# Where the adaLN weights of a two-layer diffusion step wait: rows of a transposed matrix leave the ring of raw weights for places of the general store

## The chip, the cores and the metric

The kernel runs on one core of one Trainium2 chip, in one launch. The metric is the device time of that core in microseconds (us). Five engines have queues of their own: TensorE (PE, matrix products; PEld is its weight load), VectorE (DVE), ScalarE (ACT), GpSimd (POOL) and SyncE (SP), which here does nothing but issue DMAs. Each engine takes its instructions strictly in the order in which they were written for it; an instruction that waits holds up all behind it on the same engine.

## The reference

One step of a hybrid backbone: two layers, model width 1024, 640 tokens (128 of a context, 512 of a latent grid). In each layer

```python
sh1, sc1, g1, sh2, sc2, g2 = split(silu(cond) @ w_ada + b_ada, 6)   # adaLN, two conditionings: c_ctx and c
z = (x * (1 + sc1) + sh1) @ w_in                     # one projection, cut into nine parts
r, s, n = retention(z), s5_ssm(z), attention(z)      # three mixers
m = (sig(ga) * (r @ wb[0]) + sig(gb) * (s @ wb[1]) + sig(gc) * (n @ wb[2])) @ w_o
x = layer_norm(alpha * x + g1 * m)
f = conv_ffn(x * (1 + sc2) + sh2)                    # up, 3-tap conv, gelu gate, down (D_FF = 2816)
x = layer_norm(alpha * x + g2 * f)
```

All of it is in float32. The six adaLN vectors of a layer are 48 columns of 128 numbers, for two conditionings each. The columns 0 to 15 (`sh1`, `sc1`) are needed first, 16 to 39 (`g1`, `sh2`, `sc2`) after the mixers, 40 to 47 (`g2`) after the ConvFFN.

## The kernel before, in words

**Products.** A float32 product is made as three products of rounded parts (hi·hi, hi·lo, lo·hi; `project`, L148). Weights come in tiles of 128 x 1024 (512 KB). Each is loaded by SP into one of four places of a ring called `raw` (L206), ACT rounds it to `hi` (L176), DVE subtracts to get `lo` (L177), and PE multiplies. `hi` and `lo` have rings of three places each.

**Units.** The program is a list of units that `run` goes through. A unit has slots (the weight tiles that it needs, in the order in which they are loaded) and `emit`, which writes its work. Loads are written ahead of their unit by the number of places in the ring, splits by two tiles.

**adaLN.** The first 16 columns of layer 0 are made by PE at the start. The rest is done on DVE beside other work: `ada_rows` takes 512 KB of the transposed matrix `w_adaT` (two columns of 128 outputs, one half of the 1024 inputs), and multiplies it with the conditioning, laid out as rows, in four `scalar_tensor_tensor` with a running sum (L308; the product itself goes to `junk` and is never read). There are 80 such units, spread between the products: 24 half-column units and 24 more beside the gates of each layer (L1284, L1302 and L1308 are the gate's evictions, branch products and gating), 8 and 8 for the last columns, 16 and 16 for the next layer's first columns beside layer 0's ConvFFN. Their slots are of kind `"raw"`: the tile stays in the ring of raw weights, between the weights of products, until DVE has read it four times.

**Conditioning rows.** `cond_rows` loads one half of both conditionings, broadcast over the partitions, as two tiles `crow` of 256 KB (L285), and makes silu of them with two tiles `crt` (tanh on ACT, L286; L287 and L288 on DVE). It is called again when the half changes.

**The store.** All other tiles live in a store of `NU` = 37 places of one size (`unit`, `free`): a list of idle places, taken from the front, given back at the end. A DMA into a place waits until the last reader of what lay there is done. `crow`, `crt`, the gates, q, k and v of the attention, its biases, and the tiles of the S5 preparation (`epm`, `ebe`, `eo` on POOL) come from it.

**What sets the order.** A scheduler orders each engine's instructions when the program is built; SP's queue is one in-order queue, and a DMA also waits for the one eight before it (eight semaphores take turns).

Of the kernel before, what the change touches and what calls it, by code (L numbers as in the profile page):

```python
# [11 lines left out]
FR = mybir.dt.float32r  # L12
I32 = mybir.dt.int32
AF = mybir.ActivationFunctionType
OP = mybir.AluOpType
AX = mybir.AxisListType

P = 128
# [62 lines left out]
class Kernel:  # L81
# [115 lines left out]
    def plan(s, units):  # L197
        s.units, s.cap = units, FIRST
        s.slots = [x for u in units for x in u["slots"]]
        s.raw, s.done, s.nraw, s.nsplit = {}, {}, 0, 0  # L200

    def load_to(s, n):
        while s.nraw < min(n, len(s.slots), s.cap):
            ap, kind, w = s.slots[s.nraw]
            t = s.wp.tile([P, 1024], FT, name=s.name("raw"), tag="raw", bufs=NRAW)
            s.nc.sync.dma_start(t[:, :w], ap)  # L206
            s.raw[s.nraw] = t
            s.nraw += 1

    def split_to(s, n):  # L210
        while s.nsplit < min(n, len(s.slots), s.cap):
            i = s.nsplit
            s.load_to(i + 1)
            t = s.raw.pop(i)
            w = s.slots[i][2]
            if s.slots[i][1] == "raw":
                s.done[i] = (t, None)
            else:
                hi = s.wp.tile([P, 1024], FR, name=s.name("hi"), tag="hi", bufs=NHL)
                lo = s.wp.tile([P, 1024], FR, name=s.name("lo"), tag="lo", bufs=NHL)  # L220
                s.split(hi[:, :w], lo[:, :w], t[:, :w], s.nc.gpsimd if s.slots[i][1] == "pool" else None)
                s.done[i] = (hi, lo)
            s.nsplit += 1

    def run(s, units):
        s.plan(units)
        active, at, held = [], 0, 0
        for u in units:
            n = len(u["slots"])
            s.split_to(at + n)  # L230
            s.load_to(at + n + NRAW - 1)
            for g in u.get("need", ()):
                if g in active:
                    for _ in g[1]:
                        pass
                    active.remove(g)
            tiles = [s.done.pop(at + i) for i in range(n)]
            s.mark(u)
            u["emit"](tiles)
            s.mark(None)  # L240
            at += n
            held += u.get("hold", 0)
            s.split_to(min(at + SPLIT_AHEAD, at + NHL - held))
            s.load_to(at + NRAW)
            active += u.get("start", ())
            for g in list(active):
                g[3] += g[2] * u.get("cost", 0)
                while g[3] >= 1:
                    g[3] -= 1
                    if next(g[1], "end") == "end":  # L250
                        active.remove(g)
                        break
        for g in active:
            for _ in g[1]:
                pass
# [41 lines left out]
    def ada_rows(s, l, m, i, last):  # L297

        def emit(tiles):
            nc = s.nc  # L300
            w = tiles[0][0].rearrange("p (n k) -> p n k", n=2)
            c = slice(2 * m, 2 * m + 2)
            out = s.adac[l][:, c]
            acc = s.small([P, 2, 2], "aacc", 3) if last else out
            junk = s.small([P, 512], "junk", 1, mybir.dt.bfloat16)
            for n in range(2):
                for j in range(2):
                    nc.vector.scalar_tensor_tensor(junk, w[:, n], 1.0, s.crow[j], op0=OP.mult, op1=OP.mult,  # L308
                                                   accum_out=acc[:, n, j:j + 1])
            if last:  # L310
                nc.vector.tensor_tensor(out, out, acc, op=OP.add)
                nc.vector.tensor_tensor(out, out, s.bcol[l][:, c, None].to_broadcast([P, 2, 2]), op=OP.add)
                s.ready.add((l, m))
        return dict(slots=[(s.A["w_adaT"][l, m, i], "raw", 1024)], emit=emit)

    def make_gate(s, l, which, half):

# [1442 lines left out]

NU, NRAW, NHL, SPLIT_AHEAD, LEAD = 37, 4, 3, 2, 1


@with_exitstack
def tile_hybrid_step(ctx, tc, A, O, dbg=None, layers=DEPTH):
# [93 lines left out]
```

## Time and profile before

| | |
|---|---|
| median of 3 runs | 2592.34 us (2585.28 to 2592.64) |
| profiled execution: time / span | 2584.16 us / 2582.3 us |
| PE busy | 2416.7 us (94%) |
| DVE busy | 1809.3 us (70%) |
| ACT busy | 954.7 us (37%) |
| POOL busy | 482.5 us (19%) |
| DMA | 324.04 MB, mean 125 GB/s |

Busy is the time in which an engine executed instructions that count (waits and DMA issues don't). The profiled execution is 8.2 us, or 0.3%, under the median. Times within a trace are counted from the start of the span.

### The profile page before, as it was taken

How to read it: one execution, taken by the hardware profiler on the slowest of the kernel's cores; microseconds unless marked ns; L12 is line 12 of the kernel's file. 1: busy time of each engine (PE TensorE's matmuls, PEld its weight loads, DVE VectorE, ACT ScalarE, POOL GpSimd, SP SyncE). 2: the span in 40 equal slices, each digit the busy share in tenths (PEclk: the TensorE clock that was granted, in tenths of full speed). 3: DMA queues.
4: the chain of work that ended last, by engine and by line, in shares of the span. 5: the costliest groups of instructions: out<-in, count | busy, mean ns of one | idle time of the engine just before them, and what ended most of it. 6: DMA issues, size and time to landing. Idle time of an engine off the chain costs nothing. (4 is left out here: it accounts for less than half of the span.)

```text
span 2582.3 us, 45009 instructions
## 1 busy us (share of the span) xinstructions
PE 2416.7 (94%) x17788; PEld 2342.7 (91%) x17788; DVE 1809.3 (70%) x4043; ACT 954.7 (37%) x1649; POOL 482.5 (19%) x336
## 2 busy tenths in 40 slices
PE   7879999899999997989999999989989989999997
PEld 4769999899899997979999999989988989999997
DVE  5997965785367896798665578478545788555657
ACT  3245333136543432313234543421656243232232
POOL 1555101221200007492000210102213200000001
PEclk9889999999999999999999999999999999999999
DMA  8653535552223337345335323555222343222222
GB/s 286 174 173 112 171 95 162 182 162 80 77 91 123 113 108 220 123 131 151 119 99 186 99 92 103 159 176 168 93 87 79 111 127 115 86 62 86 84 76 79
DMA packets 174083, 324.04 MB, mean 125 GB/s; under 512 B 35120, under 2 KB 84528, under 8 KB 173872
## 3 DMA queue, kind: packets, MB, share of 16 engines
q1 hardware_dynamic: 173440, 321.03, 39.5%
q8 instruction: 140, 2.29, 0.4%
q14 instruction: 71, 0.58, 0.1%
q10 hardware_dynamic: 432, 0.13, 0.0%
HBM read 287.09 MB, written 38.21 MB: 126 GB/s over the span
## 5 line engine op out<-in xcount | busy, mean ns | idle before, releaser
L148 PE MATMUL pa<-hth,hi 128*128 128x320 f32 (+2 forms) x2896 | 689.7, 316 | 49.3 <-DVE cv L1381 21.9
L148 PE MATMUL pa<-htl,hi 128*128 128x320 f32 (+2 forms) x2896 | 686.4, 315 | 1.2 <-DVE htl L461 0.8
L148 PE MATMUL pa<-hth,lo 128*128 128x320 f32 (+2 forms) x2896 | 686.0, 314 | 1.5 <-DVE lo L177 1.5
L176 ACT ACTIVATE hi<-raw 128x1024 fp32r<-128x1024 f32 (+1 forms) x316 | 322.2, 1022 | 840.9 <-PE pa L148 336.8
L177 DVE TENSOR_TENSOR lo<-raw,hi 128x1024 fp32r<-128x1024 f32 (+1 forms) x316 | 406.1, 1287 | 289.5 <-ACT hi L176 282.2
L148 PEld LDWEIGHTS pa<-hth,hi 128*128 128x128 f32 x2896 | 496.6, 192 | 59.1 <-issue 26.3
L148 PEld LDWEIGHTS pa<-htl,hi 128*128 128x128 f32 x2896 | 496.3, 191 | 9.1 <-issue 3.0
L148 PEld LDWEIGHTS pa<-hth,lo 128*128 128x128 f32 x2896 | 497.6, 192 | 7.4 <-issue 5.4
L308 DVE SCALAR_TENSOR_TENSOR junk<-raw,crow 128x512 bf16<-128x512 f32 x320 | 249.8, 781 | 53.1 <-DMA raw<-in_w_adaT 48.5
L1338 PE MATMUL b<-lo,hdh 128*128 128x256 f32 x784 | 218.8, 281 | 1.2 <-DVE lo L177 1.1
L1337 PE MATMUL b<-hi,hdh 128*128 128x256 f32 x784 | 216.7, 282 | 3.0 <-DVE rm L1341 1.9
L1339 PE MATMUL b<-hi,hdl 128*128 128x256 f32 x784 | 217.7, 281 | 0.0
L1381 DVE SCALAR_TENSOR_TENSOR cv<-pa,conv,cv 128x641 f32<-128x641 f32 (+3 forms) x180 | 153.1, 852 | 3.6 <-ACT cv L1377 1.5
L1337 PEld LDWEIGHTS b<-hi,hdh 128*128 128x128 f32 x784 | 146.1, 188 | 5.3 <-DVE rm L1341 1.8
L1338 PEld LDWEIGHTS b<-lo,hdh 128*128 128x128 f32 x784 | 147.7, 188 | 1.9 <-DVE lo L177 1.7
L1339 PEld LDWEIGHTS b<-hi,hdl 128*128 128x128 f32 x784 | 147.1, 188 | 0.2 <-issue 0.2
L1341 DVE TENSOR_TENSOR rm<-b,g 128x256 f32<-128x256 f32 x168 | 69.0, 418 | 71.9 <-PE b L1339 69.8
L431 POOL TENSOR_TENSOR x<-x,ln_b 128x512 f32<-128x512 f32 x4 | 6.5, 1660 | 521.2 <-ACT x L430 521.2
L516 PE MATMUL pa<-lo,hth 128*128 128x256 f32 x320 | 91.8, 288 | 2.7 <-DVE lo L177 2.7
L515 PE MATMUL pa<-hi,hth 128*128 128x256 f32 x320 | 93.2, 294 | 1.0 <-ACT rw L1488 1.0
L517 PE MATMUL pa<-hi,htl 128*128 128x256 f32 x320 | 91.2, 288 | 0.0
L176 ACT ACTIVATE hdh<-cv 128x641 fp32r<-128x641 f32 x44 | 32.6, 742 | 143.0 <-DVE cv L1389 132.4
(404 smaller groups left out, 4403.9 us busy)
## 6 DMA issues: line engine op xcount, KB each, us to landing
raw<-in_w_in_a SPq DMA_DIRECT2D x96, 512.0 KB
raw<-in_w_up SPq DMA_DIRECT2D x88, 512.0 KB
raw<-in_w_adaT SPq DMA_DIRECT2D x80, 512.0 KB
raw<-in_w_down SPq DMA_DIRECT2D x36, 512.0 KB
raw<-in_w_branch SPq DMA_DIRECT2D x24, 512.0 KB
raw<-in_w_o SPq DMA_DIRECT2D x24, 512.0 KB
wada<-in_w_ada SPq DMA_DIRECT2D x32, 256.0 KB
raw<-in_w_in_b SPq DMA_DIRECT2D x16, 512.0 KB
```

What stands on the lines that cost most here:

```text
L148: s.nc.tensor.matmul(ps[h][:, :n], w[a][:, k], x[b][:, k, c0:c0 + n], start=(k == 0 and part == 0), stop=(k == nk - 1 and part == 2))
L176: s.nc.scalar.activation(hi, src, AF.Copy)
L177: return (eng or s.nc.vector).tensor_tensor(lo, src, hi.bitcast(FT), op=OP.subtract)
L308: nc.vector.scalar_tensor_tensor(junk, w[:, n], 1.0, s.crow[j], op0=OP.mult, op1=OP.mult, accum_out=acc[:, n, j:j + 1])
L515: mm(ps, h[0], x[0], start=(k == 0), stop=False)
L516: mm(ps, h[0], x[1], start=False, stop=False)
L517: mm(ps, h[1], x[0], start=False, stop=(k == 7))
L1337: mm(ps, a[0], x[0], start=(k == 0), stop=False)
L1338: mm(ps, a[0], x[1], start=False, stop=False)
L1339: mm(ps, a[1], x[0], start=False, stop=(k == nk - 1))
L1341: nc.vector.tensor_tensor(m, ps, g[0 if t == 0 else 1][:, 256 * (q % 2):256 * (q % 2) + 256], op=OP.mult)
L1381: nc.vector.scalar_tensor_tensor(x[:, o0:o1], z[:, z0:z0 + o1 - o0], cw(tap), x[:, o0:o1], op0=OP.mult, op1=OP.add)
```

## The change

The rows of `w_adaT` no longer pass through the ring `raw`. A row unit has no slots any more, but an entry `rows`; a new function, `load_rows`, takes two places of the store for it and loads the two columns as two DMAs of 128 x 512 (256 KB each). `run` calls it after each unit once the first row unit has come, up to two rows ahead (`ROWS_AHEAD`), as long as six places (`ROOM`) are idle, and without that condition just before the unit that needs them. The places are given back after the four operations. The number of operations on PE, ACT, POOL and DVE stays; 80 DMAs of 512 KB become 160 of 256 KB.

```diff
+    def load_rows(s, n, must):
+        while s.rows_at < min(n, len(s.rows_in)) and (must or len(s.idle) >= ROOM):
+            ts = [s.unit([P, 512], base="arow") for _ in range(2)]
+            for i, t in enumerate(ts):
+                s.nc.sync.dma_start(t, s.rows_in[s.rows_at][:, 512 * i:512 * i + 512])
+            s.rows_of[s.rows_at] = ts
+            s.rows_at += 1
...
     def split_to(s, n):
...
-            if s.slots[i][1] == "raw":
-                s.done[i] = (t, None)
-            else:
-                hi = s.wp.tile([P, 1024], FR, name=s.name("hi"), tag="hi", bufs=NHL)
...
     def run(s, units):
...
             tiles = [s.done.pop(at + i) for i in range(n)]
+            if u.get("rows"):
+                rows += 1
+                s.load_rows(rows, True)
+                tiles = s.rows_of.pop(rows - 1)
...
             s.load_to(at + NRAW)
+            if rows:
+                s.load_rows(rows + ROWS_AHEAD, False)
...
     def ada_rows(s, l, m, i, last):
...
-                    nc.vector.scalar_tensor_tensor(junk, w[:, n], 1.0, s.crow[j], op0=OP.mult, op1=OP.mult,
+                    nc.vector.scalar_tensor_tensor(junk, tiles[n], 1.0, s.crow[j], op0=OP.mult, op1=OP.mult,
                                                    accum_out=acc[:, n, j:j + 1])
+            s.free(tiles)
...
-        return dict(slots=[(s.A["w_adaT"][l, m, i], "raw", 1024)], emit=emit)
+        return dict(slots=[], rows=[s.A["w_adaT"][l, m, i]], emit=emit)
...
+ROWS_AHEAD, ROOM = 2, 6
```

Lines behind the new function stand 10 to 15 lines lower: L206 becomes L216, L285 L298, L308 L320, L1284 L1297, L1308 L1321, L1381 L1394; L148, L176 and L177 stay.

The scheduler writes other orders for it. The first place is SP's queue in layer 0, where the gate's units begin. `raw_4738` of the change is the first weight of the gate's projection, loaded before as `raw_4881`. Before:

```order
L206 DMA raw_4817<-in_w_branch 128x1024
L726 DMA vb_5727<-nvd_2528 128x1x256
...
L206 DMA raw_4870<-in_w_adaT 128x1024
L737 DMA kc_5732<-in_cache_kT 128x1x256
L206 DMA raw_4881<-in_w_in_a 128x1024
L726 DMA vb_5721<-nvd_2528 128x1x256 x2
...
L206 DMA raw_4888<-in_w_adaT 128x1024
L726 DMA vb_5718<-nvd_2528 128x1x256
L206 DMA raw_4948<-in_w_adaT 128x1024
L206 DMA raw_4955<-in_w_in_a 128x1024
```

And in the change:

```order
L216 DMA raw_4664<-in_w_branch 128x1024
L298 DMA crow_4740<-in_c_ctx 128x512
L216 DMA raw_4738<-in_w_in_a 128x1024
L208 DMA arow_5185<-in_w_adaT 128x512
...
L208 DMA arow_4831<-in_w_adaT 128x512
L216 DMA raw_4824<-in_w_in_a 128x1024
...
L216 DMA raw_4968<-in_w_in_a 128x1024
...
L208 DMA arow_5327<-in_w_adaT 128x512
L298 DMA crow_5396<-in_c 128x512
```

The weights `raw_4738` and `raw_4824` moved ahead of the loads `vb` and `kc` of the attention, which come later now, and the rows stand behind the first weight; `crow_5396`, the second half of the conditioning, moved from ahead of these weights (as `crow_5360`) to behind them.

The second place is DVE in layer 0's ConvFFN, where the first columns of layer 1 are made (`cv` L1381, then L1394, is a convolution tap; `hdl` is the low part of its result). Before:

```order
L177 TENSOR_TENSOR lo_10805<-raw_10661,hi_10804 128x1024
L1381 SCALAR_TENSOR_TENSOR cv_10712<-pa_10663,conv_8104,cv_10712 128x640
...
L1381 SCALAR_TENSOR_TENSOR cv_10766<-pa_10717,conv_8104,cv_10766 128x640
L1381 SCALAR_TENSOR_TENSOR cv_10766<-pa_10717,conv_8104,cv_10766 128x641
L1389 TENSOR_TENSOR cv_10766<-cv_10712,cv_10766 128x641
L308 SCALAR_TENSOR_TENSOR junk_11257,adac_10371<-raw_10959,crow_9681 128x512
L308 SCALAR_TENSOR_TENSOR junk_11257,adac_10371<-raw_10959,crow_9687 128x512
L177 TENSOR_TENSOR hdl_10772<-cv_10766,hdh_10771 128x641
```

And in the change, where `cv_10786` and `cv_10840` are the same taps as `cv_10712` and `cv_10766`:

```order
L177 TENSOR_TENSOR lo_10850<-raw_10595,hi_10849 128x1024
L320 SCALAR_TENSOR_TENSOR junk_11339,adac_10443<-arow_10882,crow_9753 128x512
...
L320 SCALAR_TENSOR_TENSOR junk_11339,adac_10443<-arow_10883,crow_9759 128x512
L177 TENSOR_TENSOR lo_10854<-raw_10715,hi_10853 128x1024
L1394 SCALAR_TENSOR_TENSOR cv_10786<-pa_10737,conv_8160,cv_10786 128x640
...
L320 SCALAR_TENSOR_TENSOR junk_11490,adac_10443<-arow_11033,crow_9753 128x512
...
L320 SCALAR_TENSOR_TENSOR junk_11490,adac_10443<-arow_11034,crow_9759 128x512
L177 TENSOR_TENSOR lo_11001<-raw_10735,hi_11000 128x1024
L1394 SCALAR_TENSOR_TENSOR cv_10840<-pa_10791,conv_8160,cv_10840 128x640
```

The four operations of the row that stood behind both taps stand ahead of both now, and those of the next row between them.

The third place is DVE in layer 0's attention (`nm`, `nsm`, `pr`: maximum, sum and probabilities of a softmax, L829 to L838 before, L842 to L851 now). In the change the last row's operations stand there:

```order
L842 TENSOR_REDUCE nm_5964<-b_5948 128x1
...
L320 SCALAR_TENSOR_TENSOR junk_6233,aacc_6232<-arow_6078,crow_5390 128x512
L849 TENSOR_TENSOR nsm_5965<-nsm_5965 128x1
L320 SCALAR_TENSOR_TENSOR junk_6233,aacc_6232<-arow_6078,crow_5396 128x512
L850 RECIPROCAL nsm_5965<-nsm_5965 128x1
L842 TENSOR_REDUCE nm_5984<-b_5973 128x1
```

Before, all rows of this group were done ahead of the softmax. `arow_6078` takes a place of the store that a tile of the first attention rows gives back.

## Rows read from the trace of the kernel before

**Rows 1.** The page of the profile: busy time of the engines

```profile
PE 2416.7 (94%) x17788; PEld 2342.7 (91%) x17788; DVE 1809.3 (70%) x4043; ACT 954.7 (37%) x1649; POOL 482.5 (19%) x336
```

**Rows 2.** Who waited for whom: total us, times, longest us

```profile
ACT hi L176 <- DMA raw<-in_w_in_a: 51.1, 7, 11.3
DVE junk L308 <- DMA raw<-in_w_adaT: 48.5, 24, 11.1
...
PE pa L148 <- DVE cv L1381: 21.9, 6, 11.6
```

**Rows 3.** The same view for SP's DMA queue

```profile
SPq L206 <- DVE lo L177: 851.5, 170, 24.4
SPq L206 <- DVE junk L308: 128.8, 57, 6.3
```

**Rows 4.** Timeline of SP, layer 0's gate: start us, us, instruction

```profile
449.14 2.99 SPq L206 DMA_DIRECT2D raw<-in_w_in_a  x1
...
464.46 0.33 SPq L206 DMA_DIRECT2D raw<-in_w_in_a  x1
```

**Rows 5.** Timeline of ACT in that stretch; in brackets idle before, releaser

```profile
460.04 1.06 ACT L176 ACTIVATE hi<-raw 128x1024 fp32r<-128x1024 f32 x1 [10.23 <-DMA raw<-in_w_in_a]
461.00 1.28 ACT L1284 ACTIVATE gt<-pa 128x640 f32<-128x640 f32 x2
```

**Rows 6.** Timeline of PE in the same stretch

```profile
461.74 0.56 PE L1302 MATMUL pa<-sohi,hi 128*128 128x320 f32 x2 [2.93 <-ACT gt L1284]
...
473.43 0.57 PE L148 MATMUL pa<-hth,hi 128*128 128x320 f32 x2 [4.39 <-DVE gt L1308]
```

**Rows 7.** Timeline of SP, layer 0's ConvFFN

```profile
1013.10 0.53 SPq L206 DMA_DIRECT2D raw<-in_w_adaT  x1
```

**Rows 8.** Timeline of DVE in that stretch

```profile
1018.36 0.69 DVE L308 SCALAR_TENSOR_TENSOR junk<-raw,crow 128x512 bf16<-128x512 f32 x1 [11.06 <-DMA raw<-in_w_adaT]
...
1023.26 1.75 DVE L308 SCALAR_TENSOR_TENSOR junk<-raw,crow 128x512 bf16<-128x512 f32 x1
```

**Rows 9.** Timeline of PE, layer 0's ConvFFN, two places

```profile
1026.88 0.61 PE L148 MATMUL pa<-hth,hi 128*128 128x320 f32 x1 [11.57 <-DVE cv L1381]
...
1165.27 0.87 PE L148 MATMUL pa<-hth,hi 128*128 128x320 f32 x2 [6.61 <-DVE cv L1381]
```

**Rows 10.** Timeline of DVE ahead of the second of these places

```profile
1154.37 1.69 DVE L308 SCALAR_TENSOR_TENSOR junk<-raw,crow 128x512 bf16<-128x512 f32 x1
...
1158.04 1.90 DVE L308 SCALAR_TENSOR_TENSOR junk<-raw,crow 128x512 bf16<-128x512 f32 x1
...
1163.33 0.87 DVE L1381 SCALAR_TENSOR_TENSOR cv<-pa,conv,cv 128x640 f32<-128x640 f32 x1
```

**Rows 11.** Timeline of PE, layer 1's gate

```profile
1667.39 0.56 PE L1302 MATMUL pa<-rohi,hi 128*128 128x320 f32 x2 [3.25 <-DVE mg L1308]
...
1720.68 0.90 PE L1302 MATMUL pa<-sohi,hi 128*128 128x320 f32 x2 [5.70 <-ACT gt L1284]
...
1729.53 0.56 PE L1302 MATMUL pa<-sohi,hi 128*128 128x320 f32 x2 [3.78 <-ACT gt L1284]
```

**Rows 12.** Stretches: busy us (x instructions) by engine, granted clock, DMA share, GB/s

```profile
470.00:480.00 10.00, 6.57 (x34) 6.57 (x35) 9.12 (x14) 2.35 (x3) 4.30 (x3) 0.83 0.38 115
1000.00:1015.00 15.00, 15.00 (x103) 15.00 (x102) 5.24 (x4) 4.82 (x6) 14.82 (x12) 1.00 0.63 204
1026.90:1036.00 9.10, 9.10 (x50) 9.10 (x51) 6.48 (x10) 3.39 (x5) 5.26 (x4) 0.80 0.68 234
1100.00:1200.00 100.00, 87.02 (x787) 82.23 (x786) 89.98 (x126) 20.11 (x24) 75.21 (x44) 0.93 0.46 141
1165.30:1175.00 9.70, 9.70 (x50) 9.70 (x51) 5.56 (x9) 3.30 (x5) 3.71 (x3) 0.73 0.40 123
```

**Rows 13.** Timeline of DVE in layer 0's attention

```profile
579.43 0.48 DVE L830 CUSTOM_DVE_ANT_0 pr<-b,bias,nm 128x256 f32<-128x256 f32 x1
...
581.05 0.16 DVE L836 TENSOR_TENSOR nsm<-nsm 128x1 f32<-128x1 f32 x1 [1.12 <-ACT pr L833]
```

More of the change, by code (lines that the diff above doesn't have):

```diff
@@ L200, in plan @@
         s.raw, s.done, s.nraw, s.nsplit = {}, {}, 0, 0
+        s.rows_in, s.rows_at, s.rows_of = [x for u in units for x in u.get("rows", ())], 0, {}
+    def load_rows(s, n, must):
[5 more added lines that the diff above has]
+            s.rows_at += 1
     def load_to(s, n):
@@ L215, in split_to @@
             w = s.slots[i][2]
-            if s.slots[i][1] == "raw":
-                s.done[i] = (t, None)
-            else:
-                hi = s.wp.tile([P, 1024], FR, name=s.name("hi"), tag="hi", bufs=NHL)
-                lo = s.wp.tile([P, 1024], FR, name=s.name("lo"), tag="lo", bufs=NHL)
-                s.split(hi[:, :w], lo[:, :w], t[:, :w], s.nc.gpsimd if s.slots[i][1] == "pool" else None)
-                s.done[i] = (hi, lo)
+            hi = s.wp.tile([P, 1024], FR, name=s.name("hi"), tag="hi", bufs=NHL)
+            lo = s.wp.tile([P, 1024], FR, name=s.name("lo"), tag="lo", bufs=NHL)
+            s.split(hi[:, :w], lo[:, :w], t[:, :w], s.nc.gpsimd if s.slots[i][1] == "pool" else None)
+            s.done[i] = (hi, lo)
             s.nsplit += 1
@@ L226, in run @@
         s.plan(units)
-        active, at, held = [], 0, 0
+        active, at, held, rows = [], 0, 0, 0
         for u in units:
@@ L300, in emit @@
             nc = s.nc
-            w = tiles[0][0].rearrange("p (n k) -> p n k", n=2)
             c = slice(2 * m, 2 * m + 2)
```

## The prediction

> **What bounds the kernel now.** I read the page first: PE is busy for 2416.7 us of the span, DVE for 1809.3 [rows 1]. Only what lets PE wait can be won, so the next view is that of who waited for whom. It shows the ring's trouble twice. ACT waited 51.1 us in 7 pieces for weights of the input projection to land, up to 11.3 us at a time, and DVE 48.5 us in 24 pieces for rows of `w_adaT` [rows 2]. The same view for SP says why they landed late: beside 851.5 us in which a load waited for the split that frees its place, 128.8 us in 57 pieces went to rows not yet read by DVE [rows 3]. A row that lies in the ring keeps a weight from being asked for.
>
> Then I followed three such waits on the timelines up to PE. **Layer 0's gate:** SP issues a weight at 449.14 [rows 4]; ACT waits 10.23 us for it, and two gate evictions stand behind the split on ACT [rows 5]; PE, whose product banks are not free, idles 2.93 us, and 4.39 us a little later, when DVE has fallen behind [rows 6]. **Layer 0's ConvFFN:** SP issues a row only at 1013.10 [rows 7]; DVE waits 11.06 us for it, with a `hdl` and two convolution taps behind it [rows 8]; PE idles 11.57 us [rows 9]. The row took 5.3 us from issue to use (1013.10 to 1018.36). **Layer 1's gate** repeats layer 0's: PE idles 5.70 and 3.78 us for gate evictions behind late weights, and 3.25 us for DVE [rows 11]. A fourth idle stretch of 6.61 us [rows 9] has another cause: DVE is busy all through it, with row operations of 1.69 and 1.90 us each ahead of the tap that PE needs [rows 10].
>
> After such a pause the granted clock is lower: 0.83 from 470 to 480, 0.80 from 1026.9 to 1036, 0.73 from 1165.3 to 1175 [rows 12]; elsewhere it is 1.00, as from 1000 to 1015. By clock times length, these cost 10 x 0.17 = 1.7, 9.1 x 0.20 = 1.8 and 9.7 x 0.27 = 2.6 us.
>
> **The change part by part.** *Weights.* In layer 0's gate the first weight's place is now freed by the split of an earlier weight, not by a row, and SP issues it ahead of the rows and of the attention's loads. The two pauses, 2.93 + 4.39 us, and the clock, 1.7, make 9.0 us at most; nothing at least, if DVE, which has the same work, becomes the limit in their place. One cost is seen in the order: `crow_5396` now takes a place that row operations free, and its tanh stands on ACT ahead of the next weight splits. A tile of half a row's size should land in no more than the row's 5.3 us, and ACT had 10.23 us of idle time there. I take 7. In layer 1, 5.70 + 3.78 + two clock losses of 1.7 (taken from layer 0) make 12.9 us at most, nothing at least; I take 12, since `crow` comes later behind a weight of that gate, but still before ACT stood idle. The 3.25 us I leave.
>
> *Rows in the ConvFFN.* Rows are asked for up to two units ahead, so the row of 1013 is there in time; at most 11.57 + 1.8 = 13.4 us come back. But the scheduler also moves its four operations, and the next row's four, ahead of taps. DVE was busy for 5.24 of the 15 us before the pause [rows 12], so 9.8 us are free there. Eight operations at 0.69 us [rows 8] are 5.5 and fit. At the 1.69 to 1.90 us that they take at 1154 and 1158 [rows 10], they are about 14.4 and 4.6 do not fit; the 5.3 us of the new rows' own landing may add some 3. The stretch is nearer the second: POOL is busy for 14.82 of these 15 us [rows 12], and one of the late row's operations took 1.75 [rows 8]. I take 13.4 - 7.4 = 6; below, nothing.
>
> On this the Trainium skill has a rule ("SBUF — State Buffer", section Who interferes with whom): a VectorE instruction with two SBUF inputs shares a read port with a GpSimd instruction that reads SBUF, and the one that comes second waits for the other's end. The trace agrees as far as it goes (0.69 against 1.69 to 1.90 us). By it the eight operations cost some 14 us and not 5.5, and every place to which the order moves rows beside POOL's work would lose likewise.
>
> *The pause at 1165.* The second half's `crow` comes earlier, the tap now stands ahead of the rows, but in these 100 us DVE is busy for 89.98 [rows 12] and its work stays the same: of 6.61 + 2.6 = 9.2 us I take half, 4.6, between nothing and all.
>
> *New waits.* Places of the store can be late, too. Three rows, two in layer 0's attention and one in layer 1's, take a place that the attention itself gives back, and their operations stand between those of the softmax (579.43, 581.05 [rows 13]), for whose results PE's next products wait. Each can hold DVE for nothing, if its place is free early, up to the 5.3 us from issue to use: 0 to 16 us. DVE has gaps of about a microsecond there while it waits for ACT (1.12 [rows 13]), and PE has projections to do meanwhile, so I take 5, nearer the lower end.
>
> *Free parts.* 80 more DMA issues on SP (0.33 us for one [rows 4]) are 26 us of a queue that mostly waits. The bytes stay. The numbers of operations on PE, ACT, POOL and DVE stay. The S5 preparation's loads (`epm`, `ebe`) get their places later; POOL is idle for a quarter of the 100 us in which its results are read (75.21 busy [rows 12]), and I charge nothing; if that cover is gone, PE waits as at 1165, 6.61 us.
>
> **The sum.** 7 + 12 + 6 + 4.6 - 5 = 24.6 us. The profiled execution would come to 2584.2 - 24.6 = 2559.6; it lies 8.2 us under the median of the runs, against which I predict: 2592.3 - 24.6 = 2568.
>
> **The rivals.**
>
> (a) All pauses go: 9.0 + 12.9 + 13.4 + 9.2 = 44.5 us and no new one, 2548. For it: rows and weights stop sharing places altogether. Against: DVE keeps its work, and 90% of a stretch [rows 12] leaves it little room.
>
> (b) The port decides: the eight operations cost what POOL's neighbours cost, more rows are moved beside POOL, and nothing is won in the ConvFFN: 24.6 - 10.6 = 14 us, 2578. For it: 1.69 to 1.90 us in the trace. Against: POOL's work moves, too. The rule of the Trainium skill on the shared port (SBUF — State Buffer, Who interferes with whom) would have it so.
>
> (c) The waits change their names: ACT waits for `crow` as it did for weights, DVE for taps; 3 us in layer 0's gate and 6 in layer 1's, less 9 in the attention: 2592, no change. For it: in-order engines, and SP's queue, in which one row without a place holds up the weights behind it.
>
> (d) Slower, by the softmax: if the three late rows come as late as that at 1013 did, each costs 11.57 + 1.8 = 13.4 us, 40.2 in all, against the 29.6 won elsewhere: 2592.3 + 10.6 = 2603. It decides from 29.6 / 3, about 10 us per row, twice the time from issue to use; so their issue, too, would have to be held back.
>
> **How the numbers follow.** A measurement of this kernel can tell about 0.3%, 7.8 us, from no change. My forecast (2555 to 2576 by itself) gets 0.46, (a) 0.12, (b) 0.14, (c) 0.14, (d) 0.14. Faster is the forecast with (a) and (b), 0.72; the same is (c), 0.14; slower is (d), 0.14. The range from 2545 to 2600 takes in everything but (d) and the edge of (a).
>
> **What would show it.** Right: ACT's waits for weights of the input projection fall from 51.1 to under 10 us; the pauses of PE in both gates are gone, and DVE's 11 us for a row in the ConvFFN too, while PE still pauses some microseconds for a tap near 1000, with row operations well above 0.69 us before it; single DVE waits of 2 to 5 us for `arow` in the softmax. Wrong: ACT waits for `crow` for as long as for weights; gate pauses that only move, because DVE was the limit; POOL late with S5's tiles; or places so late that SP's row issues hold weights back.

## The result and the profile after

The change is slower: 2618.1 us (median; 2609.64 to 2629.08) against 2589.76 us of the kernel before in the same comparison (2585.28 to 2592.64), a ratio of 1.0113 with a 95% interval of 1.0071 to 1.0156. The prediction of 2568 us was wrong in sign. The profiled execution has a span of 2614.1 us (before 2582.3).

The page of the change, to be read beside [rows 1]:

```profile
span 2614.1 us, 45284 instructions
...
PE 2428.2 (93%) x17788; PEld 2350.8 (90%) x17788; DVE 1797.3 (69%) x4043; ACT 954.5 (37%) x1649; POOL 474.7 (18%) x336
```

The span grew by 31.8 us, PE's busy time by 11.5 with the same 17788 products, DVE's fell by 12.0. So no engine got more work: PE waited 20 us longer, and its products took longer.

Who waited for whom in the change, beside [rows 2] (total us, times, longest us):

```profile
ACT kch L176 <- DMA kc<-in_cache_kT: 36.8, 5, 11.2
DVE junk L320 <- DMA arow<-in_w_adaT: 34.9, 16, 8.5
ACT crt L299 <- DMA crow<-in_c_ctx: 29.4, 6, 8.2
```

ACT's 51.1 us for weights of the input projection have left the list, and DVE's wait for rows fell from 48.5 to 34.9. The first line is new. `kc` is a tile of the attention's cached keys, which comes from the store; the kernel before has no such wait.

To see where the time went, I marked in each trace when the n-th product of `project` (L148) starts, the same n in each. Lengths between marks, in us; won (+) and lost (-) are against before. `e1_near` is the first experiment below, the change with one condition more:

```
n              stage                        before  change  won     e1_near  won
1200 to 1680   layer 0's gate                115.9   102.5  +13.4    102.8   +13.1
1680 to 2400   layer 0's attention, norm     280.3   300.7  -20.4    284.7    -4.4
2400 to 4080   layer 0's ConvFFN             415.6   423.8   -8.2    423.3    -7.7
5520 to 6000   layer 1's gate                175.6   170.7   +4.9    157.4   +18.2
6000 to 6960   layer 1's attention, norm     317.7   333.4  -15.7    324.9    -7.2
               all else                                      -5.8             -2.8
```

The marks count products of L148 alone; a few of other lines can move across one. Each stage is read from one trace, and between two kernels that differ only behind the 1200th product its start alone differed by up to 4.4 us; smaller differences of one stage mean little. The gates gained, as predicted. The attentions lost 20.4 and 15.7 us, layer 0's ConvFFN 8.2.

**Layer 0's attention.** SP's queue in the change:

```profile
588.45 0.33 SPq L208 DMA_DIRECT2D arow<-in_w_adaT  x1
...
589.55 1.90 SPq L208 DMA_DIRECT2D arow<-in_w_adaT  x4
...
632.05 0.81 SPq L778 DMA_DIRECT2D bias<-in_rpb  x2
...
638.52 7.19 SPq L739 DMA_DIRECT2D vb<-nvd  x8
...
647.26 3.64 SPq L750 DMA_DIRECT2D kc<-in_cache_kT  x2
```

Five tiles of rows are loaded at 588 to 591. SP issues no further row until 871.61, and the first operation on rows after the attention is this one on DVE:

```profile
862.40 0.69 DVE L320 SCALAR_TENSOR_TENSOR junk<-arow,crow 128x512 bf16<-128x512 f32 x1
```

So four of the five lie in the store from 591 to 862 at least, 271 us, and do nothing: they are the two rows that `ROWS_AHEAD` allows, and their units come only with the ConvFFN. All that time the store has 33 places and not 37 for attention and projections. Of SP's waits from 592 to 860, these are the ones for a place of `bias`, a tile that the attention loads into the store:

```profile
SPq L778 <- PE b L769: 17.4, 1, 17.4
...
SPq L777 <- PE b L769: 9.7, 2, 9.4
```

The loads of `bias` wait until products of scores have read older tiles. `vb` and `kc` stand behind them in SP's queue. ACT and PE then pay (in brackets the idle time before, and the releaser):

```profile
659.57 0.63 ACT L176 ACTIVATE kch<-kc 128x512 fp32r<-128x512 f32 x1 [10.88 <-DMA kc<-in_cache_kT]
```

```profile
661.01 0.48 PE L769 MATMUL b<-kh,qs 128*128 128x128 f32 x1 [8.01 <-ACT kh L759]
```

`kh` stands directly behind `kch` on ACT. In stretches of the change (columns as in [rows 12]), the same place has a granted clock of 0.77; layer 0's gate with its attention, the ConvFFN, and layer 1's gate with its attention follow whole:

```profile
651.00:680.00 29.00, 18.24 (x104) 17.12 (x103) 8.76 (x30) 12.35 (x31) 1.27 (x1) 0.77 0.23 72
...
455.40:858.60 403.20, 372.96 (x2679) 354.95 (x2678) 262.27 (x615) 172.48 (x386) 56.56 (x44) 0.96 0.34 110
858.60:1282.40 423.80, 387.37 (x2919) 379.08 (x2918) 335.67 (x612) 115.66 (x141) 157.38 (x104) 0.97 0.47 143
1652.90:2157.00 504.10, 466.84 (x3325) 447.90 (x3325) 329.35 (x711) 211.12 (x434) 93.43 (x68) 0.96 0.39 122
```

### The profile page after: what moved, and what is told of

The parts are those of the page before. It is cut to its first block, busy times and chain, and to the rows that moved or that the text cites. A ratio compares the mean times of both kernels' runs of the same rounds, so it can differ in the third digit from the quotient of the medians.

```text
span 2614.1 us, 45284 instructions
## 1 busy us (share of the span) xinstructions
PE 2428.2 (93%) x17788; PEld 2350.8 (90%) x17788; DVE 1797.3 (69%) x4043; ACT 954.5 (37%) x1649; POOL 474.7 (18%) x336
## 4 chain that ended last, share of the span: by engine, by line
PE 64%; DVE 17%; DMA 8%; issue 5%; ACT 3%; POOL 3%; SPq 1%; DVEq 0%; ACTq 0%; POOLq 0%
PE pa L148 35%; DVE junk L320 4%; PE pa L1315 4%; PE b L1351 4%; PE b L1350 4%; PE b L1352 4%; DVE lo L177 3%; DMA arow<-in_w_adaT 2%; DMA kc<-in_cache_kT 2%; PE b L769 1%; PE pn L871 1%; PE pa L528 1%; PE b L858 1%; PE pa L530 1%; PE pa L529 1%
## 5 line engine op out<-in xcount | busy, mean ns | idle before, releaser
L148 PE MATMUL pa<-hth,hi 128*128 128x320 f32 (+2 forms) x2896 | 691.0, 317 | 48.7 <-DVE cv L1394 18.4
L148 PE MATMUL pa<-htl,hi 128*128 128x320 f32 (+2 forms) x2896 | 686.6, 315 | 1.2 <-DVE htl L474 0.8
L148 PE MATMUL pa<-hth,lo 128*128 128x320 f32 (+2 forms) x2896 | 683.5, 314 | 1.2 <-DVE lo L177 1.2
L177 DVE TENSOR_TENSOR lo<-raw,hi 128x1024 fp32r<-128x1024 f32 (+1 forms) x316 | 400.7, 1270 | 309.0 <-ACT hi L176 306.2
L176 ACT ACTIVATE hi<-raw 128x1024 fp32r<-128x1024 f32 (+1 forms) x316 | 322.0, 1021 | 777.3 <-PE pa L148 325.5
L148 PEld LDWEIGHTS pa<-hth,hi 128*128 128x128 f32 x2896 | 495.9, 192 | 61.3 <-issue 25.2
L148 PEld LDWEIGHTS pa<-htl,hi 128*128 128x128 f32 x2896 | 497.9, 192 | 8.8 <-issue 2.7
L148 PEld LDWEIGHTS pa<-hth,lo 128*128 128x128 f32 x2896 | 498.0, 192 | 4.6 <-issue 2.8
L320 DVE SCALAR_TENSOR_TENSOR junk<-arow,crow 128x512 bf16<-128x512 f32 x320 | 244.4, 764 | 38.9 <-DMA arow<-in_w_adaT 34.9
L1394 DVE SCALAR_TENSOR_TENSOR cv<-pa,conv,cv 128x641 f32<-128x641 f32 (+3 forms) x180 | 153.3, 853 | 4.5 <-ACT cv L1390 2.2
L176 ACT ACTIVATE hdh<-cv 128x641 fp32r<-128x641 f32 x44 | 32.7, 743 | 165.4 <-DVE cv L1402 157.8
```

Of the source, the lines that this page charges most:

```text
L148: s.nc.tensor.matmul(ps[h][:, :n], w[a][:, k], x[b][:, k, c0:c0 + n], start=(k == 0 and part == 0), stop=(k == nk - 1 and part == 2))
L176: s.nc.scalar.activation(hi, src, AF.Copy)
L177: return (eng or s.nc.vector).tensor_tensor(lo, src, hi.bitcast(FT), op=OP.subtract)
L320: nc.vector.scalar_tensor_tensor(junk, tiles[n], 1.0, s.crow[j], op0=OP.mult, op1=OP.mult, accum_out=acc[:, n, j:j + 1])
L1394: nc.vector.scalar_tensor_tensor(x[:, o0:o1], z[:, z0:z0 + o1 - o0], cw(tap), x[:, o0:o1], op0=OP.mult, op1=OP.add)
```

## The experiments

**Theory A:** the tiles loaded ahead keep places from the attention between two groups of row units. **Theory B**, the rival from the prediction: rows that come late stand between the operations of the softmax and hold up PE.

**One condition more: no row earlier than eight units before its use.** `s.rows_by` lists the row units' numbers.

```diff
-        while s.rows_at < min(n, len(s.rows_in)) and (must or len(s.idle) >= ROOM):
+        while s.rows_at < min(n, len(s.rows_in)) and (must or len(s.idle) >= ROOM and s.rows_by[s.rows_at] <= s.now + NEAR):
...
+        for s.now, u in enumerate(units):
...
+ROWS_AHEAD, ROOM, NEAR = 2, 6, 8
```

> As the change, but a row is loaded ahead only if its unit is at most 8 units away, so that no row lies in the store from one group of rows to the next (in the change, two rows, four places, lie there through each attention stage). Theory A, the places held by idle rows starve the attention (each layer's attention stage lost about 20 us against the kernel before, which ate the 13 and 8 us won in the gates): those 2 x 20 us come back, the time is about 2618 - 35 = 2583, and the pause of PE for kh (8.0 us at 653, ACT behind a late kc) shrinks to the 3.5 us of before. Theory B, the two late rows between the softmax operations and the order that the scheduler wrote: both are still there, the time stays within 8 us of the change, 2610 to 2626.

Measured: 2579.05 us, ratio 0.9963 (0.9951 to 0.9975). The change's loss is gone, 41.0 us of span (2614.1 to 2573.1). ACT's wait for `kc` is not in this trace's list, and from 560 us to the end of layer 0's attention the loads of `bias` wait 5.8 us in all, in the change 36.7. After the last tile of the gate's rows (591.57) SP issues no row before 820 here (the first of four tiles):

```profile
820.29 0.33 SPq L209 DMA_DIRECT2D arow<-in_w_adaT  x1
```

```profile
453.30:840.80 387.50, 368.14 (x2678) 351.21 (x2677) 258.60 (x615) 172.56 (x386) 56.20 (x44) 0.98 0.35 114
840.80:1264.10 423.30, 387.97 (x2918) 379.64 (x2917) 338.66 (x612) 115.36 (x141) 160.35 (x104) 0.96 0.47 142
1636.30:2118.60 482.30, 455.87 (x3302) 437.25 (x3301) 331.52 (x709) 209.55 (x431) 96.86 (x68) 0.99 0.41 128
```

In layer 0's gate and attention the change takes 403.20 us and this 387.50: of the 15.7 us, 10.9 are idle time of PE (30.2 against 19.4) and 4.8 are the same products at a lower clock (0.96 against 0.98).

One expected sign missed: PE's pause beside `kch` shrank from 8.01 us to 6.74, not to 3.5. With its keys on time ACT waits there for POOL's `kl` instead:

```profile
655.91 0.48 PE L770 MATMUL b<-kl,qs 128*128 128x128 f32 x1 [6.74 <-ACT kl L762]
```

So the late `kc` shows that places are short, but it is only 1.3 us of the price. The rest of the idle time is spread over many shorter pauses of PE in the attention.

**No rows ahead at all.**

```diff
-ROWS_AHEAD, ROOM = 2, 6
+ROWS_AHEAD, ROOM = 0, 6
```

> As the change, with no row loaded ahead of its unit (0 instead of 2). No places are held by idle rows at all. Theory A: attention stages as before, but rows are asked for later, so DVE waits for them more than the 34.9 us in total of the change; about 2590 in all. Theory B (order and late rows in the softmax): about as the change, 2610 or more.

Measured: 2596.23 us, ratio 1.0035 (1.0021 to 1.005). Up-projection to up-projection, layer 0's stretch takes 394.0 us and layer 1's 489.5 (change 403.2 and 504.1): with nothing lying idle, most of the loss there is gone, as A has it. But layer 0's ConvFFN takes 432.9 (change 423.8), and DVE's waits for rows in the whole kernel rose from 34.9 us to 54.3, as expected of rows asked for only at their unit. ACT waits for `kc` here too (23.2 us, the longest 18.25 at 529.65), but in the gates: only such waits inside an attention go with held places.

**Rows in a ring of their own,** four tiles of half a row, out of a store of 34 places.

```diff
-            ts = [s.unit([P, 512], base="arow") for _ in range(2)]
+            ts = [s.wp.tile([P, 512], FT, name=s.name("arow"), tag="arow", bufs=NROW) for _ in range(2)]
...
-NU, NRAW, NHL, SPLIT_AHEAD, LEAD = 37, 4, 3, 2, 1
+NU, NRAW, NHL, SPLIT_AHEAD, LEAD = 34, 4, 3, 2, 1
...
+ROWS_AHEAD, NROW = 1, 4
```

> As the change, but the rows have a ring of four tiles of 128 x 512 of their own, one row ahead, paid for by three places of the store (34 instead of 37); the ring of raw weights still serves products alone. Theory A (it is the number of free places that the attention lacks): three places are missing for good, so each attention stage stays 15 us or more above that of the kernel before, the gates keep what they won, about 2605 to 2625. Theory B (rows that get their places from the attention itself come late between the softmax operations): no row waits for a place of the attention any more, the stages come back, about 2585.

Measured: 2638.75 us, ratio 1.0192 (1.0168 to 1.0217). Much of it is lost before any row is read: the 1200th product starts at 491.2 us instead of 451.5. The attentions take 287.7 and 328.9 us, 7.4 and 11.2 more than before: between what A (15 or more) and B (none) expected. The smaller store costs in other stages, too, so the run alone does not decide.

**The kernel before with 33 places.**

```diff
-NU, NRAW, NHL, SPLIT_AHEAD, LEAD = 37, 4, 3, 2, 1
+NU, NRAW, NHL, SPLIT_AHEAD, LEAD = 33, 4, 3, 2, 1
```

> The kernel before with 33 places in the store instead of 37, nothing else changed. Theory A: four places fewer, as two idle rows hold them, cost each attention stage about 20 us and the S5 preparation beside layer 0's ConvFFN some more: 2589 + 40 = 2630. Theory B: the places do not matter by themselves, within 8 us of 2589.

Measured: 2681.77 us, ratio 1.0369 (1.0337 to 1.0401), more than expected. The 1200th product starts at 486.0: the store is short everywhere, also where the change holds nothing. After it, layer 0's gate and attention lose 17.5 us (413.7 against 396.2) and layer 1's 22.6. The size agrees with A, but this run cannot say that the change's places do it. The next do.

**The kernel before, with four empty places set aside** only while the change's rows lie idle in the two attentions: from unit 88 to 129 and from 283 to 324. Nothing else is changed.

```diff
+        kept = []
+        for i, u in enumerate(units):
...
+            if i in HOLD:
+                kept += [s.idle.pop(0) for _ in range(4)]
+            if i + 1 in HOLD.values():
+                s.idle += kept
+                kept = []
...
+HOLD = {88: 129, 283: 324}
```

> The kernel before, rows in the ring as ever, but four places of the store are set aside, with nothing in them, from the last row unit of each layer's gate to the first row unit behind its attention, as the change's two idle rows do. Theory A (idle rows starve the attention): each attention stage (about from 567 to 848 and from 1811 to 2128) loses some 10 to 20 us, nothing else moves; 2587 + 30 = 2617. Theory B (the attention of the change lost by its late rows and by the scheduler's order around them): no row is late here; within 8 us of 2587.

Measured: 2620.89 us, ratio 1.0144 (1.0127 to 1.0162). The kernel before, with its rows in the ring, loses as much as the change does, and ACT waits for `kc` inside the attention, as in the change. Its list of waits and ACT's timeline:

```profile
ACT kch L176 <- DMA kc<-in_cache_kT: 30.3, 4, 10.2
```

```profile
662.56 0.63 ACT L176 ACTIVATE kch<-kc 128x512 fp32r<-128x512 f32 x1 [10.19 <-DMA kc<-in_cache_kT]
```

Layer 0's gate and attention lose 14.8 us (411.0 against 396.2). Of the 36.8 us of span (2619.1 against 2582.3), 24.4 lie in the two attentions (15.0 and 9.4). The other 12.4 lie in stages where nothing is set aside, 4.9 of them in the ConvFFN; "nothing else moves" was not met, and no run says why.

**The first experiment with the same places set aside.** Diff as above, in its code.

> The first experiment (rows loaded ahead only if their unit is near, 2579 us) with the same four empty places set aside over the same two stretches. Theory A: the attention stages lose again what the first experiment gave back, about 2579 + 35 = 2614, as slow as the change. If the places do not matter there: 2579.

Measured: 2607.3 us, ratio 1.0089 (1.0072 to 1.0105). The wait is back:

```profile
ACT kch L176 <- DMA kc<-in_cache_kT: 34.0, 4, 13.1
```

Layer 0's gate and attention take 404.3 us, 16.8 more than in the first experiment; the change took 15.7 more. Layer 1's take 6.4 more, where the change took 21.8 more. So in layer 1 something was still missing.

**The third stretch set aside as well,** the one between the ConvFFN and layer 1's gate.

```diff
-HOLD = {88: 129, 283: 324}
+HOLD = {88: 129, 190: 238, 283: 324}
```

> The sixth experiment (near rows only, four empty places set aside over both attention stages: 2607 us) with the same four places set aside over the third stretch in which the change keeps two idle rows, too: from the last row beside layer 0's ConvFFN to the first row of layer 1's gate, over layer 0's down projection and layer 1's mixers. The change itself runs at 2618. Theory A in full (held places are all that separates the change from the first experiment): 2618 within 8 us, the 11 us that were missing come in the stretch around 1290 to 1660 and at the start of layer 1's gate. If something else separates them: 2607 as before.

Measured: 2623.01 us, ratio 1.0144 (1.0127 to 1.0161), where the change has 1.0113 (1.0071 to 1.0156). Layer 1's gate and attention take 502.5 us, 20.2 more than in the first experiment (change: 21.8 more). The new 13.8 us come late in the held stretch, not all along it: from the 5520th to the 5760th product the first experiment and `e6_near_hold4` take 99.7 and 99.3 us, this kernel 112.5, the change 112.6. There PE waits in this kernel for a gate, longest here:

```profile
1692.16 0.90 PE L1323 MATMUL pa<-rohi,hi 128*128 128x320 f32 x2 [10.21 <-ACT gt L1305]
```

In the change the same 112.6 us hold less idle time, 7.9 us, a granted clock of 0.95 (1.00 in the first experiment) and 23 products of other lines more. So the total is alike, and its parts are not.

**A mark in all runs.** At the head of the product with `w_o` that ends each attention, PE waits for DVE's `rm`, itself a tile of the store. The change, then the first experiment:

```profile
827.26 0.58 PE L1350 MATMUL pa<-hi,mhi 128*128 128x256 f32 x1 [4.79 <-DVE rm L1354]
```

```profile
812.55 0.38 PE L1351 MATMUL pa<-hi,mhi 128*128 128x256 f32 x1 [1.34 <-DVE rm L1355]
```

In both layers this pause is 4.79 us wherever four places are missing there (the change, the kernel before with 33 places, the three kernels with places set aside), 3.55 where three are missing (rows in a ring of their own), and 1.32 to 1.35 in all the other kernels of this document.

**The first experiment, with layer 1's first columns (the rows beside layer 0's ConvFFN) through the ring of raw weights,** as before the change. These are 16 of the 80 row units, with 64 of the 320 operations on rows; they are not 32, and not 16 and 16.

```diff
+            if s.slots[i][1] == "raw":
+                s.done[i] = (t, None)
+                s.nsplit += 1
+                continue
...
+            if ring:
+                w = tiles[0][0].rearrange("p (n k) -> p n k", n=2)
+                tiles = [w[:, 0], w[:, 1]]
...
-            r = lambda i, last: [s.ada_rows(l, m, i, last) for m in range(a // 2, b // 2)]
+            r = lambda i, last: [s.ada_rows(l, m, i, last, a == 0) for m in range(a // 2, b // 2)]
```

> The first experiment, but layer 1's first columns (the 32 rows beside layer 0's ConvFFN) go through the ring of raw weights as before; only the gates' and the last columns' rows use the store. In the first experiment this ConvFFN lost about 9 us against the kernel before (row operations at 1.65 us moved ahead of taps, rows waited for for 4.7, 2.6 and 5.4 us). If that is the cost of loading these rows through the store, they come back: about 2570, and the pause of before at 1015 (11.6 us) comes back with them at most as large. If the stretch loses for another reason: 2579.

Measured: 2564.8 us (2558.14 to 2568.23), ratio 0.9914 (0.9892 to 0.9935), faster than both kernels. The ConvFFN takes 417.9 us, 5.4 fewer than in the first experiment and 2.3 more than before; the span fell by 6.6. As expected the pause of before near 1015 is back, no larger: PE waits 9.85 us there for a tap. The page:

```profile
span 2566.5 us, 45222 instructions
...
PE 2407.4 (94%) x17788; PEld 2331.7 (91%) x17788; DVE 1806.0 (70%) x4043; ACT 955.1 (37%) x1649; POOL 483.5 (19%) x336
```

**Other depths.** The first experiment with four rows ahead; the ring version with one and with three.

```diff
-ROWS_AHEAD, ROOM, NEAR = 2, 6, 8
+ROWS_AHEAD, ROOM, NEAR = 4, 6, 8
```

> The first experiment (2579 us) with up to four rows ahead of their unit instead of two, still only near units. What is still open is why layer 0's ConvFFN loses some 9 us in it. If it is that rows there land late (DVE waited 29.8 us for them in all, 4.7, 2.6 and 5.4 us in that stretch), four ahead mends it: the stretch as before, about 2570. If it is the order, in which row operations stand ahead of taps and cost 1.65 us beside POOL, or the eight places that rows can now hold, nothing comes back or it is slower: 2579 to 2600.

Measured: 2584.76 us, ratio 0.9988 (0.9974 to 1.0002). The ConvFFN takes 436.6 us instead of 423.3: asking earlier does not cure it.

```diff
-ROWS_AHEAD, ROOM, NEAR = 2, 6, 8
+ROWS_AHEAD, ROOM, NEAR = 1, 6, 8
```

> The seventh experiment (2565 us: ConvFFN rows in the ring, the gates' rows in the store, two ahead if near) with one row ahead. If the gates' win hangs on having the weights out of the rows' way, and not on the rows being early, it stays within 8 us of 2565; if rows must be early, it loses several us in each gate: 2575 or more.

Measured: 2584.75 us, ratio 0.9982 (0.9972 to 0.9992). That rows must be early in the gates is not borne out: gate and attention take 391.5 and 483.8 us, 2.1 and 3.6 more than with two. The ConvFFN takes 427.6, 9.7 more, and its rows did not change their path.

```diff
-ROWS_AHEAD, ROOM, NEAR = 2, 6, 8
+ROWS_AHEAD, ROOM, NEAR = 3, 6, 8
```

> The seventh experiment with three rows ahead. If two are enough, and the store is short of places near the gates too, it is the same or slower, 2560 to 2580; if rows still come late with two, faster, about 2555.

Measured: 2577.56 us, ratio 0.9961 (0.9947 to 0.9974); ConvFFN 423.5. The three ring versions differ by up to 9.7 us in a stage whose rows go the same way, presumably through the order that the scheduler writes and the places that are left; no run parts the two. So the 5.4 us that the ring gave back there are not told apart from such an effect.

## Why the prediction was wrong

**The step that failed** is "New waits". It asked how long a row waits for a place that the attention gives back, priced that at 0 to 16 us and took 5. It did not ask what waits for the places that rows hold. `load_rows` counts rows, not time: after the last unit of a group it takes the next group's two rows, whose units come 41 to 48 units later. Theory A is shown from both sides. Taking the early loads away returns 41.0 us of span: 24.5 in the two attentions and 13.3 in layer 1's gate are most of it. Holding as many empty places costs the two attentions 24.4 us in the kernel before and 23.1 in the first experiment, and the third stretch costs layer 1's gate 13.2. The first experiment with all three stretches held has the change's time. Which waits of the attention make up its share is followed only in part.

Without the held places the forecast was too high still: the first experiment lies 8.4 us under the kernel before (span 9.2), not 24.6. Its gates won 31.3 us in the table where 19 were predicted, its attentions lost 11.6 where 5 were, its ConvFFN lost 7.7 where 10.6 were to be won, and all else lost 2.8.

**Theory B fell, and rival (d) with it,** though its sign was right. The rows between the softmax operations waited 1.06 and 0.85 us in layer 0 and 1.11 in layer 1, not some 10 each, on DVE's timeline in the change:

```profile
572.25 0.69 DVE L320 SCALAR_TENSOR_TENSOR junk<-arow,crow 128x512 bf16<-128x512 f32 x1 [1.06 <-DMA arow<-in_w_adaT]
...
592.54 0.74 DVE L320 SCALAR_TENSOR_TENSOR junk<-arow,crow 128x512 bf16<-128x512 f32 x1 [0.85 <-DMA arow<-in_w_adaT]
...
1851.52 0.69 DVE L320 SCALAR_TENSOR_TENSOR junk<-arow,crow 128x512 bf16<-128x512 f32 x1 [1.11 <-DMA arow<-in_w_adaT]
```

In layer 0 they stand there in the first experiment as well, which is faster.

**Weights: the mechanism was right, the sizes were off.** In layer 0's gate +7 was predicted and 13.4 measured; the two pauses of [rows 6] are gone. From 404 to 575 us PE is busy for 166.25 us, in the kernel before for 158.10:

```profile
404.00:575.00 171.00, 166.25 (x1134) 164.59 (x1133) 136.64 (x285) 55.48 (x92) 34.40 (x21) 1.00 0.52 170
```

ACT did wait for `crow`, in all 45.7 us (29.4 for `c_ctx`, 16.3 for `c`; before 17.8), which the prediction named as a sign of being wrong. But the 8.23 us at 478.82 cost nothing that PE shows: rival (c) had the new name right and not its price. For layer 1's gate +12 was predicted; the change has 4.9, and 18.2 without the held places.

**Rows in the ConvFFN: +6 was predicted, and the stage lost.** At the place itself (2880th to 3360th product: 133.2 us before, 136.4 now) the picture is near the forecast. DVE and PE in the change, beside [rows 8, 9]:

```profile
1022.00 1.43 DVE L320 SCALAR_TENSOR_TENSOR junk<-arow,crow 128x512 bf16<-128x512 f32 x1 [3.63 <-DMA arow<-in_w_adaT]
...
1023.47 1.67 DVE L320 SCALAR_TENSOR_TENSOR junk<-arow,crow 128x512 bf16<-128x512 f32 x1
...
1025.19 1.65 DVE L320 SCALAR_TENSOR_TENSOR junk<-arow,crow 128x512 bf16<-128x512 f32 x1
```

```profile
1018.52 0.87 PE L148 MATMUL pa<-hth,hi 128*128 128x320 f32 x2 [2.44 <-DVE cv L1394]
1032.58 0.87 PE L148 MATMUL pa<-hth,hi 128*128 128x320 f32 x2 [5.39 <-DVE cv L1394]
```

Two pauses of 2.44 and 5.39 us stand for one of 11.57, and most of these row operations take 1.4 to 1.7 us. But the landing still cost 3.63 us. PE's idle time in this stretch fell only from 15.0 to 14.3 us, its products took 3.9 us longer, and nothing came back. The next stretch (3360th to 3600th: 89.8 before, 97.6 now) lost most in the change. There the sentence that a row asked for two units ahead "is there in time" failed. SP, POOL and DVE:

```profile
1078.14 0.33 SPq L1089 DMA_DIRECT2D ed<-eo  x1
1079.48 1.08 SPq L208 DMA_DIRECT2D arow<-in_w_adaT  x2
```

```profile
1072.58 1.67 POOL L912 TENSOR_TENSOR eo<-epm,ebe 128x512 f32<-128x512 f32 x1 [8.55 <-DMA epm<-pd]
```

```profile
1082.35 0.69 DVE L320 SCALAR_TENSOR_TENSOR junk<-arow,crow 128x512 bf16<-128x512 f32 x1 [8.46 <-DMA arow<-in_w_adaT]
```

```profile
1084.00 0.87 PE L148 MATMUL pa<-hth,hi 128*128 128x320 f32 x2 [5.91 <-DVE cv L1394]
```

POOL waits 8.55 us for `epm`, a tile of the S5 preparation that I charged nothing under "Free parts"; SP waits for POOL's results before it can issue the stores `ed` (15.1 us in two pieces from 1055 to 1085); the row stands behind that store, a tap (1082.97, L1394) behind the row. This chain is read from one trace, not tested by a run of its own. The pause at 1165 was predicted at +4.6: the stretch that held it (3600th to 3840th) went from 50.1 to 46.0, 4.1 won; the one behind it (to 4080) lost 1.6.

**The shared port, rival (b),** gave no new cost. All 320 row operations in the change, then in the kernel before (total us, mean ns):

```profile
L320 DVE SCALAR_TENSOR_TENSOR junk<-arow,crow 128x512 bf16<-128x512 f32 x320 | 244.4, 764 | 38.9 <-DMA arow<-in_w_adaT 34.9
```

```profile
L308 DVE SCALAR_TENSOR_TENSOR junk<-raw,crow 128x512 bf16<-128x512 f32 x320 | 249.8, 781 | 53.1 <-DMA raw<-in_w_adaT 48.5
```

They cost 5.4 us less in all. In both kernels 52 of the 320 overlap with an instruction of POOL, and only those are slow: they take 1.26 us on average before and 1.15 in the change, the other 268 take 0.67 to 0.70. So no more rows were moved beside POOL. By the Trainium skill (SBUF — State Buffer, Who interferes with whom), two-input operations beside GpSimd's reads wait for a port; the traces agree (1.65 against 0.69 us), and it does not carry the result.

**What stays open:** why the ConvFFN is 2 to 21 us longer than before in every version with `NEAR`; and why the attentions lose 4.4 and 7.2 us in the first experiment, too. In layer 1 the 7.2 are idle time of PE (22.6 us against 15.4), and one pause has 5.6 of them: PE waits 9.30 us for `kl`, before 3.67 at the same place. POOL makes `kl` behind tiles of `bias`, the last of which lands late. PE, then POOL, in the first experiment:

```profile
1907.33 0.47 PE L770 MATMUL b<-kl,qs 128*128 128x128 f32 x1 [9.30 <-ACT kl L762]
```

```profile
1904.31 0.72 POOL L782 TENSOR_TENSOR bias<-bias,cst 128x256 f32<-128x256 f32 x1 [3.81 <-DMA bias<-in_rpb]
```

This, too, is read from one trace.

## What to carry to other kernels

A prefetch that draws its buffers from a shared pool is paid for by whoever else needs the pool, for as long as the data lie unread; limit it by how soon they are used and not only by how many there are, and look above all at the gaps between groups of consumers. To price such a change, follow each place from its DMA to its last reader, and ask of every long stretch which loads stand in line for a place meanwhile. To test it, set empty places aside in the old kernel: if the loss appears there, too, the missing places suffice to cause it.

## What the runs showed that I had not expected

Four places of 37, empty and unused over the two attentions, cost the kernel before 1.4%, and 33 places instead of 37 for the whole program 3.7%. In layer 0 about two thirds of the held places' cost was idle time of PE, the rest a lower granted clock after the pauses (0.77 from 651 to 680).
